# Low halves of the local attention's keys stored in both row halves, and the decode tokens' copies of 1/rms tied behind the sixth attention block

## The chip, the cores and the metric

The kernel runs on one core of one Trainium2 chip. Its time is the device time of one execution in microseconds (us). A program is timed in several runs, and the median is given. TensorE is PE in the profile (its weight loads are PEld), VectorE is DVE, ScalarE is ACT, GpSimd is POOL, and SyncE, which issues most DMAs, is SP.

## The reference, cut to what matters

One layer of a hybrid decoder: 1024 prompt tokens and 64 decode tokens (8 sequences of 8) share one input projection. Half of it feeds a retention mixer, half a sliding-window attention of 8 query heads and 2 key heads (64 wide, window 128). Output projection, residual and an MLP follow. The change touches only the attention.

```python
q_s = rms_norm(q_s.reshape(b, t, N_SWA_HEADS, HEAD_DIM), q_norm_gain)
k_s = rms_norm(k_s.reshape(b, t, N_SWA_KV, HEAD_DIM), k_norm_gain)
v_s = v_s.reshape(b, t, N_SWA_KV, HEAD_DIM)
...
# swa_prompt: each block of 128 queries reads its own and the previous block of keys
scores = jnp.einsum('bnqkgd,bnskd->bnkgqs', qb, kk).astype(jnp.float32) * (d ** -0.5)
scores = scores - slopes * dist.astype(jnp.float32)
scores = jnp.where(valid[None, :, None, None], scores, NEG_INF)
probs = sink_softmax(scores, sinks).astype(v.dtype)
out = jnp.einsum('bnkgqs,bnskd->bnqkgd', probs, vv)
```

## The kernel before, in words

**Numbers in two halves.** Most products are made of a high half in the type `fp32r` and a low half, the rest. The helper `mm3` (L178 to L180) issues three matmuls for one product: high by high, low by high, high by low. A matmul of the profile shows as rows*columns of its stationary operand, then the output: `128*128 128x256` has 128 rows of contraction, `64*128` only 64.

**The key and value stage.** For each of nine token tiles `proj_tok` issues 24 matmuls of 256 columns into `pst`. ACT squares the key part (`hsq`, L313), DVE sums and scales it (`hr`, L315, L316), POOL takes the power (`hr`, L132), DVE multiplies (L318) and makes the normed keys `kn` (L320), and PE transposes them (`ptk`, L325). For tiles 0 to 7 the transposed keys are split for each of two key heads `kv`: ACT writes the high half twice, into rows 64*kv and following and into the other 64 rows (`kh2`, L331), and DVE writes the low half once, into the rows of its own head (`kl`, L332). DVE also stores the values (L335). PSUM has two buffers for `ptk`, and three for `pst`. While this runs, PE also has the second query projection (`psq`) in its order.

**The spread of 1/rms.** When the third `rst` is known (L132), SP sends all 1088 values of 1/rms to DRAM (`r_d`, L171, L172) and loads them back into all 128 partitions (`rsb`, L173). The projections of the next stage multiply by `rsb` (L515, L524). For the decode tokens DVE makes eight small copies of one row of `rsb` (`r8s`, in the tile `q2v`, L431), which are read only by the column sums `prq8` after the attention of the prompt. In the code they stand behind the eighth attention block.

**The attention blocks.** `swa_block(c)` runs for eight blocks of 128 queries and for both key heads. `qx` holds the high half of the queries in the rows of the head (`qx[p_]`, ACT L392) and their low half in the other 64 rows (DVE L393). For each of four query heads two matmuls make the scores in one part of a PSUM bank `scp`: L400 multiplies all 128 rows of `qx` by `kh2` (high by high and low by high at once), and L401 adds the 64 high rows times the low half of the keys. DVE adds the position term (L402), the softmax follows (DVE L351 to L365, ACT L359, POOL L366), PE transposes the result (`ppp`, L371), ACT and DVE copy it out (L411, L413), PE multiplies by the values (`po`, L420), and ACT and DVE split the result (L423, L424) for the output projection.

**Order.** The program is traced in the order of the code, and a scheduler then places each engine's instructions with the times of a model; the order of an engine is fixed before the run. Between the matmuls of the attention it places those of the next projections (`psf`, `psg`), which need nothing of the attention.

Of the kernel before, what the change touches and what calls it, by code (L numbers as in the profile page):

```python
# [11 lines left out]
F32 = mybir.dt.float32  # L12
F32R = mybir.dt.float32r
AF = mybir.ActivationFunctionType
ALU = mybir.AluOpType
# [5 lines left out]
P = 128  # L21
WARM = 18
T = 1088
NB = 8
# [5 lines left out]
def tok_tile(t):  # L30
    off = 960 if t == 8 else t * 128
    c = min(off // 384, 2)
    return off, c, off - CH[c][0]
# [3 lines left out]
def hymba_layer(ctx: ExitStack, tc: tile.TileContext, a: dict, o: dict):  # L37
    nc = tc.nc
# [9 lines left out]
    def slot(i, dt, name):  # L48
        return slots.tile([P, 3072], dt, tag=f"s{i}", name=name)
# [8 lines left out]
    def cload(name):  # L58
        t_ = const.tile(list(a[name].shape), F32, name="c_" + name)
        nc.sync.dma_start(t_, a[name])  # L60
        return t_
# [43 lines left out]
    qkg = cload("qkg")  # L105
# [25 lines left out]
    def rsqrt_inplace(ap, n):  # L131
        nc.gpsimd.tensor_tensor(ap, ap, mhalf.broadcast_to([P, n]), ALU.pow)  # L132
# [68 lines left out]
    rsb = nt.tile([P, T], F32, tag="rsb", name="rsb", bufs=1)  # L201
# [5 lines left out]
    def proj_tok(t, w, ps):  # L207

        _, c, r = tok_tile(t)
        hi, lo = hn[c]  # L210
        for k in range(8):
            lh, ll = hi[:, k, r : r + 128], lo[:, k, r : r + 128]
            mm3(ps[:, :256], lh, ll, w[0][:, k, :], w[1][:, k, :], k == 0, k == 7)
        return ps


    sp = attn.enter_context(tc.tile_pool(name="swa", bufs=2))
# [15 lines left out]
    sl7, sl8 = slot(7, F32, "q2v"), None  # L233
    qs2 = sl7[:, 0:1024].rearrange("p (j n) -> p j n", j=4)
    vs = sl7[:, 1024:2048].rearrange("p (t n) -> p t n", t=8)
    q8s, r8s = (sl7[:, i : i + 512].rearrange("p (t n) -> p t n", t=4) for i in (2048, 2560))
# [60 lines left out]
        square_sum(rsb[:, 768:1088], xs[2][:, k, :], k, "m2")  # L297
    sl8 = slot(8, F32R, "kk")
    kh2 = [sl8[:, kv * 1024 : kv * 1024 + 1024] for kv in range(2)]
    kl = sl8[:, 2048:3072]  # L300
    for c, (c0, cw) in enumerate(CH):
        acc = rsb[:, c0 : c0 + cw]
        inv_rms(acc, OFFS[c], rst[:, 3 * c : 3 * c + 3], f"m{c}")
# [4 lines left out]
    for t in range(9):  # L308
        off, c, r0 = tok_tile(t)
        rt = rst[:, t : t + 1]  # L310
        ps = proj_tok(t, w, psA.tile([P, 512], F32, tag="mm", name="pst"))
        sq = sp.tile([P, 128], F32, tag="hsq", name="hsq")
        nc.scalar.activation(sq, ps[:, :128], AF.Square, scale=rt)  # L313
        r = sp.tile([P, 2], F32, tag="hr", name="hr")
        nc.vector.tensor_reduce(r, sq.rearrange("p (h d) -> p h d", h=2), AX.X, ALU.add)  # L315
        nc.vector.tensor_scalar(r, r, 1.0 / 64.0, EPS, ALU.mult, ALU.add)  # L316
        rsqrt_inplace(r, 2)
        nc.vector.tensor_scalar(r, r, rt, None, ALU.mult)  # L318
        kn = sp.tile([P, 128], F32, tag="kn", name="kn")
        nc.vector.tensor_tensor(  # L320
            kn.rearrange("p (h d) -> p h d", h=2), ps[:, :128].rearrange("p (h d) -> p h d", h=2),
            r.unsqueeze(2).broadcast_to([P, 2, 64]), ALU.mult,
        )
        pt = psB.tile([P, 512], F32, tag="t2", name="ptk")[:, :128]
        nc.tensor.transpose(pt, kn, ident)  # L325
        if t < 8:
            cols = slice(t * 128, t * 128 + 128)
            for kv in range(2):
                p_ = slice(kv * 64, kv * 64 + 64)
                for d_ in (p_, slice(64 - kv * 64, 128 - kv * 64)):  # L330
                    nc.scalar.activation(kh2[kv][d_, cols], pt[p_], AF.Copy, scale=qkg[p_, 1:2])  # L331
                nc.vector.scalar_tensor_tensor(  # L332
                    kl[p_, cols], pt[p_], qkg[p_, 1:2], kh2[kv][p_, cols].bitcast(F32), ALU.mult, ALU.subtract
                )
            nc.vector.tensor_scalar(vs[:, t, :], ps[:, 128:256], rt, None, ALU.mult)  # L335
        if t == 7:
            nc.vector.tensor_scalar(k8[:, 0:128], pt, qkg[:, 1:2], None, ALU.mult)
        if t == 8:
            nc.vector.tensor_scalar(k8[:, 128:192], pt[:, 64:128], qkg[:, 1:2], None, ALU.mult)
            nc.vector.tensor_scalar(v8, ps[64:128, 128:256], rt[64:128], None, ALU.mult)  # L340
# [27 lines left out]
    def transposed(s, j0, n, nm):  # L368
        pp = psB.tile([P, 512], F32, tag="t2", name="pp" + nm)
        for g in range(4):  # L370
            nc.tensor.transpose(pp[:n, g * 128 : g * 128 + 128], s[:, g, j0 : j0 + n], ident)  # L371
        return pp

    def mix_store(mh, ml, t0, n):
        for d_, m_ in ((ms_hi_d, mh), (ms_lo_d, ml)):
            nc.sync.dma_start(d_[:, :, t0 : t0 + n], m_[:, : 4 * n].bitcast(F32).rearrange("p (g n) -> p g n", g=4))


    def swa_block(c):
        pts = []  # L380
        mh = sp.tile([P, 512], F32R, tag="mh", name=f"mh{c}")
        ml = sp.tile([P, 512], F32R, tag="ml", name=f"ml{c}")
        k0 = max(c - 1, 0) * 128
        n = 128 if c == 0 else 256
        for kv in range(2):
            nm = f"p{c}_{kv}"
            p_ = slice(kv * 64, kv * 64 + 64)
            x_ = slice(64 - kv * 64, 128 - kv * 64)

            qx = sp.tile([P, 4, 128], F32R, tag="qx", name="qx" + nm)  # L390
            q_ = qs01[p_, :, c * 128 : c * 128 + 128] if c < 6 else qs2[p_, :, c * 128 - 768 : c * 128 - 640]
            nc.scalar.copy(qx[p_], q_)  # L392
            nc.vector.tensor_tensor(qx[x_], q_, qx[p_].bitcast(F32), ALU.subtract)  # L393
            st = sp.tile([P, 4, 256], F32, tag="s", name="s" + nm)
            s = st[:, :, 256 - n :]
            for gg in range(2):
                ps = psB.tile([P, 512], F32, tag="t1", name="sc" + nm)
                for g in (2 * gg, 2 * gg + 1):
                    pg = ps[:, (g % 2) * 256 : (g % 2) * 256 + n]
                    nc.tensor.matmul(pg, qx[:, g, :], kh2[kv][:, k0 : k0 + n], start=True, stop=False)  # L400
                    nc.tensor.matmul(pg, qx[p_, g, :], kl[p_, k0 : k0 + n], start=False, stop=True)  # L401
                    nc.vector.scalar_tensor_tensor(  # L402
                        s[:, g, :], dtab[:, 256 - n :], nsl[:, c, kv, g : g + 1], pg, ALU.mult, ALU.add
                    )
            softmax(s, n, sinks[:, 4 * kv : 4 * kv + 4], nsinks[:, 4 * kv : 4 * kv + 4], nm, rq[:, c, kv, :])
            halves = (1,) if c == 0 else (0, 1)
            pt = sp.tile([P, 2, 512], F32, tag="pt", name="pt" + nm)
            for h in halves:
                pp = transposed(st, h * 128, 128, nm)
                if h == 0:  # L410
                    nc.scalar.copy(pt[:, h, :], pp)  # L411
                else:
                    nc.vector.tensor_copy(pt[:, h, :], pp)  # L413
            pts.append(pt)

        po = psB.tile([P, 512], F32, tag="t3", bufs=1, name=f"po{c}")
        for h in halves:
            for kv in range(2):
                p_ = slice(kv * 64, kv * 64 + 64)
                nc.tensor.matmul(  # L420
                    po[p_, :], vs[:, c - 1 + h, p_], pts[kv][:, h, :], start=h == halves[0], stop=h == 1
                )
        nc.scalar.copy(mh, po)  # L423
        nc.vector.tensor_tensor(ml, po, mh.bitcast(F32), ALU.subtract)  # L424
        mix_store(mh, ml, c * 128, 128)

    for c in range(NB):
        swa_block(c)

    for c_ in range(8):  # L430
        nc.vector.tensor_copy(  # L431
            r8s[0:1, :, :].rearrange("p t (b c i) -> p t b c i", b=2, c=8)[:, :, :, c_, :],
            rsb[0:1, 1024:1088].rearrange("p (t b i) -> p t b i", t=4, b=2),
        )


    pr = psB.tile([P, 512], F32, tag="t2", name="prq8")
# [25 lines left out]
    for tt in range(2):  # L463
        ps = psB.tile([P, 512], F32, tag="t1", name="sc8")
        for t4 in (2 * tt, 2 * tt + 1):
            cc = (t4 % 2) * 192
            for new in range(2):
                for b2 in range(2):
                    b = 2 * t4 + b2
                    for kv in range(2):  # L470
                        p_ = slice(kv * 64, kv * 64 + 64)
# [12 lines left out]
    for h, n in ((0, 128), (1, 64)):  # L484
        pp = transposed(s8, h * 128, n, "s")
        pt = nt.tile([P, 512], F32, tag="ntmp", name=f"pt8{h}")
# [11 lines left out]
    mh = sp.tile([P, 512], F32R, tag="mh", name="mhs")  # L498
    ml = sp.tile([P, 512], F32R, tag="ml", name="mls")
# [375 lines left out]
    kh, kl = (sl8c[:, i : i + 512].rearrange("p (q n) -> p q n", q=4) for i in (2048, 2560))  # L875
# [372 lines left out]
```

## Time and profile before

| what | us |
|---|---|
| median of 3 runs | 1283.24 (1282.28 to 1283.95) |
| the profiled execution's own time | 1280.67 |
| its span | 1278.9 |
| PE busy in the span | 1221.7 (96%) |
| DVE, ACT, POOL busy | 838.3, 499.8, 545.7 |

A timeline row gives start, duration, engine, line, operation, names, shape and count, and in brackets how long the engine sat idle before it and what ended that. Matmuls are pipelined, so the distance from start to start, not the duration, is what one costs PE; that distance is called the pitch below. PEclk is the granted clock of TensorE, 1.00 being full speed. A row of windows gives for each engine its busy time and its number of instructions in a stretch.

### The profile page before, as it was taken

What the parts mean: (1) busy time and instruction counts of PE and PEld (TensorE: products, weight loads), DVE (VectorE), ACT (ScalarE), POOL (GpSimd) and SP (SyncE); (2) the same over time, 40 slices, a digit from 0 to 9 for tenths busy, and PEclk for the clock granted to TensorE, in tenths of its full rate; (3) what the DMA queues carried; (4) which work ended last, traced back from release to release, by engine and by line L of the source; (5) the groups of instructions that cost most, each with busy time, mean ns of one, the idle gap of its engine ahead of it and who ended that gap; (6) DMA issues with size and microseconds to landing.
All of it is one profiled execution on the core that took longest, in us unless ns stands there. A gap on an engine that the chain in (4) does not pass through costs nothing.

```text
span 1278.9 us, 23839 instructions
## 1 busy us (share of the span) xinstructions
PE 1221.7 (96%) x9621; PEld 1156.2 (90%) x9621; DVE 838.3 (66%) x1492; ACT 499.8 (39%) x1031; POOL 545.7 (43%) x463
## 2 busy tenths in 40 slices
PE   7979999999999899879999999999589999999998
PEld 5979877788979799879999999999589999999998
DVE  8735655553115787887666666766367778887766
ACT  6333343364304334444444344434264332332331
POOL 8425223123323554667565656665571321413000
PEclk9989999999989999899999999999889999999999
DMA  6211221424402944332443434333575455553124
GB/s 229 68 56 53 85 74 61 156 73 135 121 18 89 301 152 148 113 113 85 154 152 131 146 143 155 139 133 140 188 262 178 137 171 157 180 181 122 55 69 175
DMA packets 97669, 169.45 MB, mean 133 GB/s; under 512 B 11487, under 2 KB 67743, under 8 KB 97303
## 3 DMA queue, kind: packets, MB, share of 16 engines
q1 hardware_dynamic: 85783, 125.46, 29.0%
q10 hardware_dynamic: 9216, 33.56, 8.1%
q0 software_dynamic: 2560, 8.91, 2.2%
q8 instruction: 75, 1.23, 0.4%
q14 instruction: 35, 0.29, 0.1%
HBM read 114.30 MB, written 53.61 MB: 131 GB/s over the span
## 4 chain that ended last, share of the span: by engine, by line
PE 75%; DVE 9%; DMA 7%; POOL 3%; issue 3%; ACT 2%; SPq 0%; ACTq 0%; DVEq 0%; POOLq 0%
PE psd L179 8%; PE psd L180 8%; PE psd L178 8%; PE psx L178 4%; PE psx L180 4%; PE psx L179 4%; PE psf L180 3%; PE psf L178 3%; PE psf L179 3%; POOL rt L1063 2%; DMA u_d<-rt 2%; PE pst L178 2%; PE psz L178 2%; PE psz L180 2%; PE psz L179 2%
## 5 line engine op out<-in xcount | busy, mean ns | idle before, releaser
L178 PE MATMUL psd<-uh,wd_w 128*128 128x272 f32 x896 | 259.5, 290 | 17.7 <-ACT uh L754 17.7
L179 PE MATMUL psd<-uh,wd_w 128*128 128x272 f32 x896 | 260.0, 291 | 0.1
L180 PE MATMUL psd<-ul,wd_w 128*128 128x272 f32 x896 | 256.7, 289 | 0.8 <-DVE ul L755 0.8
L178 PEld LDWEIGHTS psd<-uh,wd_w 128*128 128x128 f32 x896 | 170.8, 191 | 18.1 <-ACT uh L754 18.1
L179 PEld LDWEIGHTS psd<-uh,wd_w 128*128 128x128 f32 x896 | 169.7, 189 | 0.3 <-DVE wd_w L755 0.3
L180 PEld LDWEIGHTS psd<-ul,wd_w 128*128 128x128 f32 x896 | 168.7, 189 | 1.1 <-DVE ul L755 1.1
L1118 DVE TENSOR_TENSOR a<-a,psd 128x272 f32<-128x272 f32 x248 | 102.2, 432 | 46.8 <-PE psd L180 46.7
L755 DVE TENSOR_TENSOR wu_w<-wu_s,wu_w 128x512 fp32r<-128x512 f32 x64 | 62.1, 973 | 84.6 <-ACT wu_w L754 84.4
L755 DVE TENSOR_TENSOR ul<-ur,uh 128x1088 fp32r<-128x1088 f32 x56 | 87.5, 1591 | 15.2 <-ACT uh L754 15.2
L754 ACT CAST wd_w<-wd_s 128x512 fp32r<-128x512 f32 x64 | 37.6, 621 | 112.9 <-PE psd L180 101.7
L178 PE MATMUL psx<-op_0h,wu_w 128*128 128x272 f32 x256 | 75.1, 293 | 0.7 <-ACT m L1040 0.7
L366 POOL TENSOR_TENSOR sp<-sp,ssp 128x1024 f32<-128x1024 f32 (+1 forms) x16 | 28.6, 1789 | 109.9 <-DVE ssp L365 109.9
L180 PE MATMUL psx<-op_0l,wu_w 128*128 128x272 f32 x256 | 74.3, 290 | 0.0
L178 PE MATMUL psx<-op_1h,wu_w 128*128 128x272 f32 x256 | 74.3, 290 | 0.0
L180 PE MATMUL psx<-op_1l,wu_w 128*128 128x272 f32 x256 | 74.1, 289 | 0.0
L179 PE MATMUL psx<-op_0h,wu_w 128*128 128x272 f32 x256 | 74.0, 289 | 0.0
L179 PE MATMUL psx<-op_1h,wu_w 128*128 128x272 f32 x256 | 73.7, 288 | 0.0
L754 ACT CAST uh<-ur 128x1088 fp32r<-128x1088 f32 x56 | 59.5, 1101 | 22.9 <-DMA ur<-u_d 12.4
L962 POOL TENSOR_TENSOR wd_s<-wd_r,wd_s 128x512 f32<-128x512 f32 x16 | 24.0, 1501 | 104.0 <-DVE wd_w L755 101.7
L1027 DVE SCALAR_TENSOR_TENSOR m<-m,rsf 128x272 f32<-128x272 f32 x96 | 65.5, 683 | 3.1
L180 PE MATMUL psf<-hnl,wqk_hi 128*128 128x384 f32 (+1 forms) x192 | 64.9, 338 | 0.0
L178 PE MATMUL psf<-hnh,wqk_hi 128*128 128x384 f32 (+1 forms) x192 | 64.8, 338 | 0.0
(318 smaller groups left out, 3818.8 us busy)
## 6 DMA issues: line engine op xcount, KB each, us to landing
u_d<-rt SPq DMA_DIRECT2D x32, 952.0 KB, 6.1
ur<-u_d SPq DMA_DIRECT2D x56, 544.0 KB, 5.0
wu_r<-in_w_up ACTq DMA_DIRECT2D x32, 512.0 KB, 4.3
wd_r<-in_w_down ACTq DMA_DIRECT2D x32, 512.0 KB, 5.9
y<-in_xY POOLq DMA_DIRECT2D x16, 272.0 KB, 3.3
y_d<-y POOLq DMA_DIRECT2D x16, 272.0 KB, 3.7
yt<-y_d SPq DMA_DIRECT2D x16, 272.0 KB, 3.3
out_yT<-a SPq DMA_DIRECT2D x16, 272.0 KB, 2.2
```

The source lines that it names most:

```text
L178: nc.tensor.matmul(ps, lh, rh, start=first, stop=False, skip_group_check=more)
L179: nc.tensor.matmul(ps, ll, rh, start=False, stop=False, skip_group_check=more)
L180: nc.tensor.matmul(ps, lh, rl, start=False, stop=last, skip_group_check=more)
L366: nc.gpsimd.tensor_tensor(s, s, ss.unsqueeze(2).broadcast_to([P, 4, n]), ALU.mult)
L754: nc.scalar.copy(hi, src)
L755: lo_eng.tensor_tensor(lo, src, hi.bitcast(F32), ALU.subtract)
L962: nc.gpsimd.tensor_tensor(t_, p_, q_, op)
L1027: nc.vector.scalar_tensor_tensor(t_, src, 0.0, rsf[:, s, h, :], ALU.max, ALU.mult)
L1063: sub = lambda o_, p_, q_: nc.gpsimd.tensor_tensor(o_, p_, q_, ALU.subtract)
L1118: nc.vector.tensor_tensor(to, to, ps, ALU.add)
```

## The change

Three edits. First, the low halves of the keys get a tile of 128 rows for each key head (`kl2`; the second is a new tile of 4 KB in each partition), and DVE writes each low half twice, as ACT does with the high half. Second, L401 multiplies all 128 rows of `qx` by it; so the product of low by low, which was left out before, is added. Third, the eight copies L431 are put behind the last DVE instruction of the sixth block, by an order on DVE alone and without a semaphore.

```diff
-    kl = sl8[:, 2048:3072]
+    kl2 = [sl8[:, 2048:3072], sp.tile([P, 1024], F32R, tag="kl", name="kl", bufs=1)]
...
                 for d_ in (p_, slice(64 - kv * 64, 128 - kv * 64)):
                     nc.scalar.activation(kh2[kv][d_, cols], pt[p_], AF.Copy, scale=qkg[p_, 1:2])
-                nc.vector.scalar_tensor_tensor(
-                    kl[p_, cols], pt[p_], qkg[p_, 1:2], kh2[kv][p_, cols].bitcast(F32), ALU.mult, ALU.subtract
-                )
+                    nc.vector.scalar_tensor_tensor(
+                        kl2[kv][d_, cols], pt[p_], qkg[p_, 1:2], kh2[kv][p_, cols].bitcast(F32), ALU.mult, ALU.subtract
+                    )
...
                     nc.tensor.matmul(pg, qx[:, g, :], kh2[kv][:, k0 : k0 + n], start=True, stop=False)
-                    nc.tensor.matmul(pg, qx[p_, g, :], kl[p_, k0 : k0 + n], start=False, stop=True)
+                    nc.tensor.matmul(pg, qx[:, g, :], kl2[kv][:, k0 : k0 + n], start=False, stop=True)
...
-        nc.vector.tensor_tensor(ml, po, mh.bitcast(F32), ALU.subtract)
+        ins = nc.vector.tensor_tensor(ml, po, mh.bitcast(F32), ALU.subtract)
         mix_store(mh, ml, c * 128, 128)
-
-    for c in range(NB):
-        swa_block(c)
-
-    for c_ in range(8):
-        nc.vector.tensor_copy(
-            r8s[0:1, :, :].rearrange("p t (b c i) -> p t b c i", b=2, c=8)[:, :, :, c_, :],
-            rsb[0:1, 1024:1088].rearrange("p (t b i) -> p t b i", t=4, b=2),
-        )
+        return ins
+
+    done_swa = [swa_block(c) for c in range(NB)]
+    with tc.issue_after(done_swa[5].ins):
+        for c_ in range(8):
+            nc.vector.tensor_copy(
+                r8s[0:1, :, :].rearrange("p t (b c i) -> p t b c i", b=2, c=8)[:, :, :, c_, :],
+                rsb[0:1, 1024:1088].rearrange("p (t b i) -> p t b i", t=4, b=2),
+            )
```

In DVE's order of before, in the key and value stage, the copies L431 stand around the first steps of token tile 4 (L315 to L320 are its norm, `q2v<-pst` its values, `kk<-ptk` low halves of keys):

```order
L332 SCALAR_TENSOR_TENSOR kk<-ptk,c_qkg,kk 64x128
L431 COPY q2v<-rsb 1x8x8 x4
L315 TENSOR_REDUCE hr<-hsq 128x2
L431 COPY q2v<-rsb 1x8x8 x4
L316 TENSOR_SCALAR hr<-hr 128x2
L332 SCALAR_TENSOR_TENSOR kk<-ptk,c_qkg,kk 64x128
L318 TENSOR_SCALAR hr<-hr,rst 128x2
L320 TENSOR_TENSOR kn<-pst,hr 128x128
L335 TENSOR_SCALAR q2v<-pst,rst 128x128
```

The same place in DVE's order of the change, token tile 4 again:

```order
L315 TENSOR_REDUCE hr<-hsq 128x2
L332 SCALAR_TENSOR_TENSOR kk<-ptk,c_qkg,kk 64x128
L316 TENSOR_SCALAR hr<-hr 128x2
L332 SCALAR_TENSOR_TENSOR kl<-ptk,c_qkg,kk 64x128
L332 SCALAR_TENSOR_TENSOR kk<-ptk,c_qkg,kk 64x128
L318 TENSOR_SCALAR hr<-hr,rst 128x2
L320 TENSOR_TENSOR kn<-pst,hr 128x128
L335 TENSOR_SCALAR q2v<-pst,rst 128x128
L332 SCALAR_TENSOR_TENSOR kl<-ptk,c_qkg,kk 64x128
```

The copies are gone from here, and four writes of low halves (`kk` and `kl`) stand for each token tile where two stood. On ACT the number of writes is the same, but each now has one of DVE's behind it on the same PSUM tile. In PE's order 206 matmuls stand between the first and the ninth transpose `ptk` in both kernels, 144 of 256 columns (`pst`) and 62 of 384 (`psq`); the transposes stand a little further apart, the last three more so.

The place in DVE's order of the change where the copies now stand is behind L424 of the sixth block; L353 and L402 belong to the two blocks behind it, and `gst` is a projection:

```order
L351 TENSOR_REDUCE mxp_1_1974<-sp_1_1959 128x4
L424 TENSOR_TENSOR ml_1806<-po_1899,mh_1805 128x512
L431 COPY q2v<-rsb 1x8x8 x8
L353 TENSOR_TENSOR mxp_1_1974<-mxp_1_1974,rq 128x4
L413 COPY ptp_0_1943<-ppp_0_1950 128x512
L402 SCALAR_TENSOR_TENSOR sp_0_2016<-dtab,nsl,scp_0_2017 128x256
```

All eight stand together there, with the softmax of a later block behind them. Behind the attention the orders of all engines are nearly the same as before; SP's stores and loads in the attention change places among each other.

## The prediction

> **What bounds the kernel now.** I read the busy shares and the chain of waits first, to see which engine carries the end, then windows of the two places that the edits touch, and there the waits and the timeline.
>
> ```profile
> PE 1221.7 (96%) x9621; PEld 1156.2 (90%) x9621; DVE 838.3 (66%) x1492; ACT 499.8 (39%) x1031; POOL 545.7 (43%) x463
> PE 75%; DVE 9%; DMA 7%; POOL 3%; issue 3%; ACT 2%; SPq 0%; ACTq 0%; DVEq 0%; POOLq 0%
> 60.00:80.00 20.00, 13.35 (x97) 13.15 (x96) 7.98 (x36) 7.09 (x20) 2.79 (x4) 0.83 0.08 29
> 75.03:79.46 4.43, 4.43 (x21) 4.43 (x22) 3.25 (x14) 2.55 (x7) 1.39 (x2) 0.52 0.01 4
> 100.00:320.00 220.00, 220.00 (x1367) 179.36 (x1366) 118.22 (x278) 89.50 (x214) 70.11 (x33) 1.00 0.28 93
> ```
>
> The first line is the page's busy times, the second its chain by engine, the rest windows (length, then PE, PEld, DVE, ACT, POOL, granted clock, DMA). PE is the bound: 96% busy and 75% of the chain. In the attention, 100 to 320 us, it is busy in all 220 us while DVE has 118, so time saved on PE there is time saved. In the key and value stage there is a hole: 13.35 of 20 us, and just behind it a clock of 0.52.
>
> **The hole.** A row of waits (total, times, longest) and timeline rows.
>
> ```profile
> PE ptk L325 <- DVE kn L320: 6.7, 1, 6.7
> 72.38 0.49 DVE L431 COPY q2v<-rsb 1x64 f32<-1x64 f32 x4 [9.21 <-DMA rsb<-r_d]
> 106.00 0.56 DVE L515 TENSOR_TENSOR qkst<-psf,rsb 128x384 f32<-128x384 f32 x1 [0.73 <-PE psf L180]
> 67.98 0.28 PE L179 MATMUL pst<-wkv_hi,hnl 128*128 128x256 f32 x1
> 68.10 0.28 PE L180 MATMUL pst<-wkv_lo,hnh 128*128 128x256 f32 x1
> 75.03 0.47 PE L325 MATMUL ptk<-c_ident,kn 128*128 128x128 f32 x1 [6.65 <-DVE kn L320]
> 75.16 0.56 PE L178 MATMUL pst<-wkv_hi,hnh 128*128 128x256 f32 x1
> 79.49 0.36 PE L180 MATMUL pst<-wkv_lo,hnh 128*128 128x256 f32 x1
> ```
>
> DVE works in order, and L431 stands there 9.2 us until the 1/rms come back from DRAM. Behind it are queued the norm and `kn` of token tile 4, for which PE's transpose waits: PE starts nothing from 68.10 to 75.03. The third edit takes L431 out of this place. Nothing else there needs `rsb`: its next reader, L515, stands behind the whole stage (at 106.00 before, where `rsb` had landed by 72.38). What is late next is the norm itself, weighed below.
>
> The gain: from 68.10 to 79.49 are 11.4 us. The window from 75.03 holds 21 PE instructions, one the transpose; 20 matmuls of 256 columns at the pitch of 0.12 us (67.98 to 68.10) plus one for 68.10 are 2.5 us, two transposes some 0.2. **11.4 - 2.7 = 8.7 us**: 6.7 of waiting and 2.0 of half speed. That the clock comes back too is safe only if no other hole opens.
>
> **The 64-row matmul.** Timeline of PE in the attention, with its weight loads below:
>
> ```profile
> 182.73 0.33 PE L180 MATMUL psf<-hnl,wqk_hi 128*128 128x384 f32 x1
> 182.91 0.34 PE L178 MATMUL psf<-hnh,wqk_hi 128*128 128x384 f32 x1
> 183.08 0.28 PE L400 MATMUL scp<-kk,qxp 128*128 128x256 f32 x1
> 183.29 0.38 PE L401 MATMUL scp<-kk,qxp 64*128 64x256 f32 x1
> 183.60 0.45 PE L179 MATMUL psf<-hnh,wqk_lo 128*128 128x384 f32 x1
> 183.88 0.28 PE L400 MATMUL scp<-kk,qxp 128*128 128x256 f32 x1
> 184.09 0.38 PE L401 MATMUL scp<-kk,qxp 64*128 64x256 f32 x1
> 184.40 0.45 PE L180 MATMUL psf<-hnl,wqk_hi 128*128 128x384 f32 x1
> 184.69 0.34 PE L178 MATMUL psf<-hnh,wqk_hi 128*128 128x384 f32 x1
> 182.91 0.19 PEld L400 LDWEIGHTS scp<-kk,qxp 128*128 128x128 f32 x1
> 183.29 0.18 PEld L401 LDWEIGHTS scp<-kk,qxp 64*128 64x128 f32 x1 [0.19 <-issue]
> 183.60 0.19 PEld L179 LDWEIGHTS psf<-hnh,wqk_lo 128*128 128x128 f32 x1
> L401 PE MATMUL scp<-kk,qxp x64: 323/380/383, 103.0 to 293.1; 64*128 64x256 f32 x56, 64*128 64x128 f32 x8
> ```
>
> The load of L400 starts at 182.91, a matmul ahead of its use; the 64-row load of L401 and the full one behind it start only with their own matmuls. So L400 holds 0.21 us where full-height neighbours of 256 columns take 0.12, L401 0.31, and the 384-column matmul behind 0.28 to 0.29 where 0.175 is usual (182.73 to 182.91). From 183.08 to 184.69 are 1.61 us for four matmuls of 256 columns and two of 384; at the usual pitch 4 x 0.12 + 2 x 0.175 = 0.83. The excess is 0.78 for two, **0.39 us for each L401**, and there are 64 (last row): **25.0 us**. With `kl2` all are 128 rows high. The gain lies between 0 (the price stays) and 25; I take all of it, since the nearest rows are those of `pst`, 256 columns, full height, 0.12 apart with loads as long as here.
>
> The Trainium skill, on "TensorE: Matmul & The Clock Gate", in "Why this matters for your kernels", holds that a single matmul of few rows of contraction takes as long as one of 128. By that the second edit would be worth nothing and the sum only 8.7 us; the trace differs, since L401 holds PE for 0.31 us where 0.12 is usual.
>
> **What is added.** 16 more L332, and each key tile's four writes on ACT now alternate with four on DVE, since both read one PSUM tile and wait for each other:
>
> ```profile
> 57.01 0.74 ACT L331 ACTIVATE kk<-ptk,c_qkg 64x128 fp32r<-64x128 f32 x2 [2.66 <-PE ptk L325]
> 57.78 0.34 DVE L332 SCALAR_TENSOR_TENSOR kk<-ptk,c_qkg,kk 64x128 fp32r<-64x128 f32 x1 [0.28 <-ACT kk L331]
> 58.16 0.74 ACT L331 ACTIVATE kk<-ptk,c_qkg 64x128 fp32r<-64x128 f32 x2 [0.41 <-DVE kk L332]
> 61.30 0.70 POOL L132 TENSOR_TENSOR hr<-hr,mhalf 128x2 f32<-128x2 f32 x1 [3.48 <-DVE hr L316]
> 62.98 0.37 ACT L313 ACTIVATE hsq<-pst,rst 128x128 f32<-128x128 f32 x1 [0.40 <-PE pst L180]
> L335 DVE TENSOR_SCALAR q2v<-pst,rst 128x128 f32<-128x128 f32 x6 | 2.1, 342 | 0.0
> L320 DVE TENSOR_TENSOR kn<-pst,hr 128x128 f32<-128x128 f32 x7 | 2.0, 292 | 0.6
> L315 DVE TENSOR_REDUCE hr<-hsq 128x2 f32<-128x128 f32 x6 | 1.7, 277 | 2.2 <-ACT hsq L313 2.1
> L318 DVE TENSOR_SCALAR hr<-hr,rst 128x2 f32<-128x2 f32 x7 | 1.6, 229 | 2.4 <-POOL hr L132 2.3
> L431 DVE COPY q2v<-rsb 1x64 f32<-1x64 f32 x8 | 1.0, 175 | 9.2 <-DMA rsb<-r_d 9.2
> ```
>
> A step is 0.37 on ACT, 0.35 on DVE and 0.04 for each handover (57.75 to 57.78, 58.12 to 58.16): 0.80, so 3.2 us for the four of a tile. PE's own work is 144 x 0.12 + 62 x 0.175 + eight transposes at some 0.1 = 28.9 us for the eight tiles, 3.6 each. The rest of DVE's work on a tile (0.34, 0.29, 0.28, 0.23 and L316, as small as L318: 1.3 to 1.4 us) and ACT's `hsq` (0.37) fall in the other engine's turns. So the chain stays 0.4 us a tile shorter than PE's work: cost **0**. From the other side, if nothing overlaps at all, a tile takes 3.2 + 1.4 + 0.37 + 0.70 on POOL = 5.6 us, and eight take 45, **16 us** more than PE's work. I take 0, since tiles overlap in the order; 16 goes into the range. Behind the waiting writes stands the next tile's norm, hence PE's transpose.
>
> The copies L431 cost 1.0 us in their new place. Behind them there stand L353 and L413 of a later block; DVE is idle for some 46% of that stretch (118 of 220), so 0 to 1.0, taken as 0. Their reader, the column sums, comes a block and a half later.
>
> **Does the attention keep up?** A PE that is faster by 25 us over 16 rounds gets 1.6 us earlier in each to what the other engines make.
>
> ```profile
> 192.05 1.90 POOL L366 TENSOR_TENSOR sp<-sp,ssp 128x1024 f32<-128x1024 f32 x1 [6.11 <-DVE ssp L365]
> 199.76 0.49 PE L371 MATMUL ppp<-c_ident,sp 128*128 128x128 f32 x3
> PEld scp L400 <- DVE ptp L413: 0.8, 1, 0.8
> PEld scp L400 <- DVE sp L402: 0.8, 1, 0.8
> ```
>
> The softmax is ready at 193.95, and PE takes it at 199.76, 5.8 us later; 1.6 us less leaves most. Waits of PE's loads for DVE in the attention are two of 0.8 us; I add as much again, **1.6 us**, with bounds 0 and 25 (all the gain turns into waiting).
>
> **Sum.** 25.0 + 8.7 - 1.6 = 32.1 us. The profiled execution took 1280.67, so it becomes 1248.6; it lies 2.6 below the median of 1283.24, and with the same offset the forecast is **1251**.
>
> **Rivals.**
> 1. The chain of ACT and DVE becomes the bound of the key stage. For it: eight handovers a tile where four were, and POOL in the norm. Against: 3.2 against 3.6 us. Up to 16 us: 1257 to 1267.
> 2. The attention's chain takes PE's place. For it: the order was made by a model, not by this trace. Against: 5.8 us in hand. Half the gain lost gives 1251 + 12 = 1263, all of it 1276.
> 3. The edit of the scores does not do what it says: the price belongs to the pair, not to the 64 rows. For it: L400 and L401 share a bank and a stationary operand. Against: no other full-height pair shows it. Only the hole is won: 1283.2 - 8.7 + 1.6 = 1276. The Trainium skill's rule on few rows, above, leads here too.
> 4. Slower than before. Two full loads on the same rows cannot overlap a running matmul: each waits for the end of the matmul before (0.28) and then loads (0.19), 0.47 for each of the pair, and 0.28 + 0.19 = 0.47 again before the next one instead of 0.175. That is an excess of 2 x 0.35 + 0.3 = 1.0 for each pair, 0.61 above now, 39 us in all, less 8.7: some 1313. It decides from an excess above 0.39 + 8.7/64 = 0.53 us. Against: `pst` at 0.12. The same page of the Trainium skill, in "Part 3: Packing small matmuls" under "What overlaps and what doesn't", says that loads overlap running matmuls only where the row groups differ; by that rule this rival would hold. The trace disagrees: loads of 0.19 us on all 128 rows keep a pitch of 0.12.
>
> **How the numbers follow.** Forecast 0.74 (1246 to 1257), first rival 0.10, second 0.08, third 0.05, fourth 0.02, the rest, with no change, 0.01. The low end, 1246, is the full gain without the 1.6 us, 1249.5, less the scatter of runs and some pairs with an excess of 0.41; the high end, 1267, takes in the first rival's bound and the milder half of the second. About 0.2% (2.6 us) is what a measurement of this kernel can tell from no change: faster 0.97, same 0.01, slower 0.02.
>
> **What would show it.** Right: L431 no longer waits, the transposes `ptk` wait for less than 1 us each, the clock stays at 1.00 from 60 to 95 us, L401 reads 128*128, and pairs stand 0.12 apart. Wrong on the first term: a new wait of PE for `kn` in the same stage. Wrong on the second: a pitch above 0.2 at L401, or new waits of L400, L371 and L420 in the attention. What would make the whole wrong is a later stage that now ends on a DMA and gives back the lead.

## The result, and the profile after

| | us |
|---|---|
| before, median of 4 runs | 1282.76 (1281.40 to 1283.95) |
| after, median of 4 runs | 1253.33 (1252.94 to 1255.31) |
| ratio | 0.9774, 95% interval 0.9757 to 0.9791 |
| profiled execution, before and after | 1280.67 and 1253.02 |

The kernel is 29.4 us faster by the medians and 27.65 by the two profiled executions; the forecast was 1251, from a sum of 32.1. The busy times and the chain of the page after:

```profile
PE 1198.9 (96%) x9621; PEld 1151.8 (92%) x9621; DVE 841.5 (67%) x1508; ACT 504.4 (40%) x1035; POOL 545.3 (44%) x463
PE 59%; DMA 6%; DVE 5%; POOL 4%; ACT 3%; issue 2%; ACTq 0%; SPq 0%; POOLq 0%; DVEq 0%
```

Two windows of after, with the columns of the prediction's:

```profile
60.00:80.00 20.00, 20.00 (x156) 19.96 (x155) 14.60 (x50) 12.31 (x31) 7.30 (x7) 1.00 0.12 36
100.00:320.00 220.00, 216.35 (x1519) 191.89 (x1518) 121.54 (x285) 102.87 (x235) 80.70 (x42) 0.99 0.33 104
```

PE issues as many instructions as before in 22.8 us less of busy time. The key stage has no hole any more (20.00 of 20 us at full clock, against 13.35 at 0.83). From 100 to 320 us PE is no longer busy throughout: 3.65 of 220 us are idle, 1.9 of them behind the attention, at 313 us. Groups of after: the copies, the transposes of the keys and the last products of the decode tokens' attention (count, then ns min/median/max, first and last start):

```profile
L431 DVE COPY q2v<-rsb x8: 174/176/177, 247.3 to 248.0; 1x64 f32<-1x64 f32 x8
L325 PE MATMUL ptk<-c_ident,kn x9: 270/271/327, 56.6 to 85.4; 128*128 128x128 f32 x9
L495 PE MATMUL po<-pt,smp x32: 222/223/243, 309.0 to 309.9; 128*64 128x32 f32 x32
```

The timeline of PE in after, at two pairs of scores:

```profile
172.31 0.28 PE L400 MATMUL scp<-kk,qxp 128*128 128x256 f32 x1
172.43 0.28 PE L401 MATMUL scp<-kl,qxp 128*128 128x256 f32 x1
172.55 0.28 PE L400 MATMUL scp<-kk,qxp 128*128 128x256 f32 x1
172.67 0.28 PE L401 MATMUL scp<-kl,qxp 128*128 128x256 f32 x1
172.78 0.31 PE L180 MATMUL psf<-hnl,wqk_hi 128*128 128x320 f32 x1
```

The copies stand at 247 us and wait for nothing. The pairs stand 0.12 us apart, and a projection follows after another 0.11: the height of 64 rows and its price are gone.

The same two groups of before tell how the gain grows along the way:

```profile
L325 PE MATMUL ptk<-c_ident,kn x9: 270/272/473, 56.6 to 94.0; 128*128 128x128 f32 x9
L495 PE MATMUL po<-pt,smp x32: 222/223/243, 336.9 to 337.8; 128*64 128x32 f32 x32
```

After is 8.6 us ahead at the last transpose (94.0 to 85.4) and 27.9 at the last L495, with 20 more matmuls of the value projection (2.4 us) already done by then: 30.3. Of that some is given up at once. Three of PE's waits between 40 and 420 us (what waited, for whom, us in total, times, longest):

```profile
PE pst L178 <- ACT vtr L578: 2.3, 2, 1.9
PE po L420 <- ACT ptp L411: 1.1, 1, 1.1
PE scp L400 <- DVE sp L402: 0.5, 2, 0.3
```

The timeline of after at the first of these, and the window around it:

```profile
312.92 1.20 ACT L578 ACTIVATE vtr<-pst,rst 128x256 f32<-128x256 f32 x3 [2.34 <-DMA ms_hi_d<-mhs]
313.45 0.39 PE L178 MATMUL pst<-wv_hi,hnh 128*128 128x256 f32 x1 [1.91 <-ACT vtr L578]
314.26 0.41 PE L178 MATMUL pst<-wv_hi,hnh 128*128 128x256 f32 x1
314.47 0.42 PE L179 MATMUL pst<-wv_hi,hnl 128*128 128x256 f32 x1
```

```profile
310.00:320.00 10.00, 8.09 (x58) 7.85 (x55) 0.42 (x1) 2.05 (x5) 3.19 (x5) 0.83 0.72 203
```

Two more in this stretch, of `rsr` for `qkb`, are 3.4 us, and 3.6 in before; one of 1.8 us, of `pso` for the weights `woa`, does not come back in a second profiled execution of the change. The waits of the attention for ACT and DVE are 1.6 us, none in before. Behind the attention the first copies of the values (`vtr`, L578) wait for the store `ms_hi_d` to read `mhs`, whose memory they take over; the three `pst` buffers are full, PE waits 1.9 us, and some 15 matmuls behind it run 0.21 apart instead of 0.12, another 1.4 us. In before the same copies waited 3.02 us for a store and PE only 0.19.

### The profile page after: what moved, and what is told of

It is laid out like the page before. It is cut to its first block, busy times and chain, and to the rows that moved or that the text cites. A ratio compares the mean times of both kernels' runs of the same rounds, so it can differ in the third digit from the quotient of the medians.

```text
span 1251.2 us, 23864 instructions
## 1 busy us (share of the span) xinstructions
PE 1198.9 (96%) x9621; PEld 1151.8 (92%) x9621; DVE 841.5 (67%) x1508; ACT 504.4 (40%) x1035; POOL 545.3 (44%) x463
## 4 chain that ended last, share of the span: by engine, by line
PE 59%; DMA 6%; DVE 5%; POOL 4%; ACT 3%; issue 2%; ACTq 0%; SPq 0%; POOLq 0%; DVEq 0%
PE psd L179 9%; PE psd L180 9%; PE psd L178 9%; PE psx L178 3%; PE psx L179 3%; PE psx L180 3%; DMA u_d<-rt 3%; POOL rt L1063 3%; PE psz L180 2%; PE psz L179 2%; PE psz L178 2%; PE pst L178 1%; PE pst L179 1%; PE pso L179 1%; PE pso L180 1%
## 5 line engine op out<-in xcount | busy, mean ns | idle before, releaser
L366 POOL TENSOR_TENSOR sp<-sp,ssp 128x1024 f32<-128x1024 f32 (+1 forms) x16 | 28.6, 1787 | 100.4 <-DVE ssp L365 95.7
L754 ACT CAST uh<-ur 128x1088 fp32r<-128x1088 f32 x56 | 59.5, 1099 | 21.7 <-DMA ur<-u_d 11.3
```

Of the source, the lines that this page charges most:

```text
L366: nc.gpsimd.tensor_tensor(s, s, ss.unsqueeze(2).broadcast_to([P, 4, n]), ALU.mult)
L754: nc.scalar.copy(hi, src)
```

## The experiments

All ratios are to the kernel before, which was timed anew beside each group of runs: 1282.77 us beside each edit alone, the writes in pairs and the first kernel with other memory; 1281.66 beside the zero half, the grouped rows, the writes twice and the pairs with other memory; 1284.25 beside the last two. These three lie up to 2.6 us apart, and a difference in us between kernels of two groups can be off by as much. Line numbers in the rows of an experiment can be a few above those of the change.

### Each edit alone

The first two edits without the third: the copies go back behind the last block.

```diff
-    done_swa = [swa_block(c) for c in range(NB)]
-    with tc.issue_after(done_swa[5].ins):
-        for c_ in range(8):
+    for c in range(NB):
+        swa_block(c)
+    for c_ in range(8):
```

> The first two edits alone; the copies L431 stay where they were. My theory (both prices are separate and add up): the hole of 6.65 us with its 2 us of half clock stays, and the change's 29.4 us shrink by some 8.7, so 1261 to 1264, a ratio of 0.983 to 0.985 to the kernel before; L431 waits some 9 us for rsb again. Rival (the copies matter little, since the keys' low halves now keep DVE busy there anyway, or the lead is lost later as it was behind the attention): 1253 to 1256. Rival (the hole was the greater part): above 1268.

Measured: 1257.87 us, ratio 0.9801 (0.9784 to 0.9818), 24.9 us less than before. Then the third edit alone:

```diff
-                    nc.tensor.matmul(pg, qx[:, g, :], kl2[kv][:, k0 : k0 + n], start=False, stop=True)
+                    nc.tensor.matmul(pg, qx[p_, g, :], kl[p_, k0 : k0 + n], start=False, stop=True)
```

> The third edit alone; low halves and L401 as before. My theory: 8.4 to 8.7 us go at the end of the key stage and stay gone, 1274 (ratio 0.993); L401 still 64*128, with an excess of 0.35 to 0.39 us each. Rival (the lead is given back later, in the attention's waits or behind it): 1279 to 1282. If the two edits need each other, this run and the one with the rows alone do not add up to the change's 29.4 us.

Measured: 1273.33 us, ratio 0.9921 (0.9901 to 0.9940), 9.4 us less. Two waits in the key stage of the first of the two:

```profile
PE pst L178 <- DVE q2v L335: 6.7, 1, 6.7
DVE q2v L432 <- DMA rsb<-r_d: 9.1, 1, 9.1
```

Its window of that stage, and its groups of the transposes and of the decode tokens' last products:

```profile
60.00:80.00 20.00, 13.28 (x98) 12.99 (x97) 8.83 (x37) 6.22 (x18) 2.09 (x3) 0.86 0.09 28
```

```profile
L325 PE MATMUL ptk<-c_ident,kn x9: 270/272/415, 57.1 to 95.4; 128*128 128x128 f32 x9
L496 PE MATMUL po<-pt,smp x32: 222/223/243, 315.6 to 316.5; 128*64 128x32 f32 x32
```

The same window of the copies alone, and its group L401:

```profile
60.00:80.00 20.00, 20.00 (x156) 19.96 (x155) 12.15 (x41) 13.60 (x35) 7.79 (x7) 1.00 0.14 48
```

```profile
L401 PE MATMUL scp<-kk,qxp x64: 323/380/383, 94.0 to 285.0; 64*128 64x256 f32 x56, 64*128 64x128 f32 x8
```

With the copies in their old place the hole is back to the tenth of a microsecond, and with it the lower clock; with the copies moved and the low halves as before, the hole is gone and the 64-row matmuls are there. So each price belongs to its edit. But 24.9 + 9.4 = 34.3 us, and the change has 29.4: **together they lose some 4.9 us** that each alone does not. (Each of the three has an interval of some 2 us to either side, and in its second timing, below, the change has 30.4; so the loss is clear, its size is not sharp.) The rows alone came out 3 to 6 us faster than expected. From the last transpose to the last L495 it takes 221.1 us, the change 224.5; 1.6 of these 3.4 us are 13 more matmuls of the value projection that the change does by then.

The traces show where the two edits lose it. The last transposes of the retention stage, in the kernel before, the change, the rows alone and the copies alone:

```profile
L734 PE MATMUL pm<-c_ident,mixtok x4: 222/222/272, 490.6 to 490.8; 64*128 64x64 f32 x4
L734 PE MATMUL pm<-c_ident,mixtok x4: 222/222/273, 465.7 to 465.9; 64*128 64x64 f32 x4
L735 PE MATMUL pm<-c_ident,mixtok x4: 222/222/272, 470.1 to 470.3; 64*128 64x64 f32 x4
L734 PE MATMUL pm<-c_ident,mixtok x4: 222/222/273, 484.5 to 484.7; 64*128 64x64 f32 x4
```

By then PE has done the same matmuls in the last three, and in before 25 fewer of the output projection (3.1 us at 0.125). So the leads are 28.0 us for the change, 23.6 for the rows and 9.2 for the copies, and 23.6 + 9.2 - 28.0 = 4.8: in these executions the loss is complete here, nearly 800 us ahead of the end. Most of it lies behind the attention. From the last L495 to this point the rows alone take 153.8 us, the change 156.0 although it has the 1.6 us of projections behind it: 3.8 us more.

### Is it the height of the operand?

The other half of each `kl2` is filled with zeros once, and DVE writes the low halves once, as before the change:

```diff
+    for kv in range(2):
+        x_ = slice(64 - kv * 64, 128 - kv * 64)
+        nc.scalar.activation(kl2[kv][x_], rsb[x_, 0:1024], AF.Copy, scale=0.0)
...
-                    nc.vector.scalar_tensor_tensor(
-                        kl2[kv][d_, cols], ...
+                nc.vector.scalar_tensor_tensor(
+                    kl2[kv][p_, cols], ...
```

> The change, but the other row half of each kl2 holds zeros, written once by ACT ahead of the stage, and DVE writes each low half once, as before the change. So the product of low by low is left out, as it was before. L401 reads 128 rows. My theory (the price hangs on the height of L401's operands, not on what is in them, and the 16 added writes are not what the gain costs or brings): L401 stands 0.12 us from its neighbours, and the time is between that of the change and that of the writes in pairs, 1248 to 1254. Rival (the added writes hold up the key stage): below 1247. Rival (the price has to do with the data or with a tile shared by both heads): the 0.35 to 0.39 us for each L401 come back, 1270 or more.

Measured: 1249.59 us, ratio 0.9744 (0.9723 to 0.9765). Its timeline on PE, where L403 and L404 are L400 and L401; the next projection starts at 125.23:

```profile
125.00 0.28 PE L403 MATMUL scp<-kk,qxp 128*128 128x256 f32 x1
125.11 0.28 PE L404 MATMUL scp<-kk,qxp 128*128 128x256 f32 x1
```

Zeros do as well as numbers: L401 wins by having 128 rows, not by what is in them. Then the 64-row matmuls of before, with the third edit, but two of a kind behind each other:

```diff
+                for g, pg in pgs.items():
+                    nc.tensor.matmul(pg, qx[:, g, :], kh2[kv][:, k0 : k0 + n], ...)
+                for g, pg in pgs.items():
+                    nc.tensor.matmul(pg, qx[p_, g, :], kl[p_, k0 : k0 + n], ...)
```

> The third edit with L401 of 64 rows as before the change, but the four matmuls of a bank stand as L400, L400, L401, L401 instead of L400, L401, L400, L401; the computation is the same. It stands against the copies alone (1273.3 us). Theory A (the price is that of a change of height, from 128 to 64 rows and back, some 0.39 us for each way there and back): half the changes, so 12 us less, 1260 to 1263. Theory B (the price is that of every matmul with 64 rows): no difference, 1272 to 1275. The pitch in the trace tells too: by A the second L401 of a pair stands 0.12 us behind the first, by B 0.2 to 0.31.

Measured: 1262.01 us, ratio 0.9838 (0.9812 to 0.9865), 11.3 us less than the copies alone, or 10.2 with each held against its own timing of before. (Unlike what the expectation says, the attention scores are changed. The sums of the two heads of a bank are begun one inside the other here, and part of them is probably lost by that, which is not shown. Number, size and kind of the instructions are the same.) Its timeline on PE; L402 is L401 here, and a row x2 is two matmuls:

```profile
172.74 0.34 PE L178 MATMUL psf<-hnh,wqk_hi 128*128 128x384 f32 x1
172.91 0.40 PE L400 MATMUL scp<-kk,qxp 128*128 128x256 f32 x2
173.24 0.50 PE L402 MATMUL scp<-kk,qxp 64*128 64x256 f32 x2
173.66 0.44 PE L179 MATMUL psf<-hnh,wqk_lo 128*128 128x384 f32 x1
173.94 0.33 PE L180 MATMUL psf<-hnl,wqk_hi 128*128 128x384 f32 x1
```

The second 64-row matmul by itself, and its load:

```profile
173.46 0.28 PE L402 MATMUL scp<-kk,qxp 64*128 64x256 f32 x1
173.34 0.19 PEld L402 LDWEIGHTS scp<-kk,qxp 64*128 64x128 f32 x1
```

From 172.91 to 173.94 are 1.03 us; at the usual pitch, 4 x 0.12 + 0.175, it would be 0.66. The excess is 0.37 for two 64-row matmuls, where the prediction found 0.78. **Two 64-row matmuls behind each other cost together what one alone costs**, so the price is not one for each of them, and theory A has the time (12 us expected, 10 to 11 measured). Its sign in the trace is not there, though: by A the second should stand 0.12 us behind the first, and it stands 0.22 behind (173.24 to 173.46), as B has it. The excess is spread over the stretch, some 0.1 us on each of four starts. What a third in the row would cost no run shows.

### Do the added writes cost?

Half as many handovers between ACT and DVE, with the same instructions:

```diff
                 for d_ in (p_, slice(64 - kv * 64, 128 - kv * 64)):
                     nc.scalar.activation(kh2[kv][d_, cols], ...)
+                for d_ in (p_, slice(64 - kv * 64, 128 - kv * 64)):
                     nc.vector.scalar_tensor_tensor(kl2[kv][d_, cols], ...)
```

> The change, but for each key head ACT writes both high halves and then DVE both low halves, so the engines change places half as often on each PSUM tile; the same instructions otherwise. My theory (the chain of ACT and DVE is hidden behind PE in the key stage): the same time, 1252 to 1255, and the key stage's last transpose within 0.5 us of the change's 85.6 us. Rival (the handovers cost PE something): 1 to 3 us faster, and seen before 90 us.

Measured: 1248.32 us, ratio 0.9731 (0.9717 to 0.9746), 5.0 us less than the change, with intervals that don't meet. Both theories missed: it is faster, but not in the key stage. Its windows of the key stage and of the attention, then the change's own window of the attention:

```profile
60.00:80.00 20.00, 20.00 (x159) 19.96 (x158) 15.40 (x52) 13.25 (x34) 6.01 (x7) 1.00 0.12 33
100.00:310.00 210.00, 209.96 (x1438) 186.34 (x1436) 120.38 (x281) 96.19 (x228) 75.26 (x38) 1.00 0.31 100
```

```profile
100.00:310.00 210.00, 208.26 (x1467) 184.04 (x1465) 121.12 (x284) 100.82 (x230) 77.51 (x38) 1.00 0.31 99
```

The groups of transposes and last products with the writes in pairs:

```profile
L325 PE MATMUL ptk<-c_ident,kn x9: 270/271/327, 57.5 to 86.5; 128*128 128x128 f32 x9
L496 PE MATMUL po<-pt,smp x32: 222/223/243, 306.0 to 306.9; 128*64 128x32 f32 x32
```

The last transpose comes 1.1 us later than in the change and the last L495 3.0 earlier, with 13 fewer matmuls of the value projection done by then (1.6 us). PE is as busy in the key stage as can be in both. In the attention PE has 0.04 us idle here and 1.7 in the change: the scheduler laid out another order, in which the waits for `sp` and `ptp` don't arise. More is won behind it. The last transposes of the retention stage, with the same matmuls done on PE as in the change:

```profile
L735 PE MATMUL pm<-c_ident,mixtok x4: 222/222/273, 459.7 to 459.9; 64*128 64x64 f32 x4
```

That is 6.0 us ahead of the change: 1.1 lost in the key stage, 2.5 won in the attention (220.4 us against 222.9 without the 1.6) and 4.6 between the last L495 and this point (153.0 against 157.6 with them). The two profiled executions end 3.1 us apart, so part of it is given back later there. The sum of the two edits alone, 34.3 us, is what this order gives (1282.77 - 1248.32 = 34.4). Then the writes twice:

```diff
-                    nc.vector.scalar_tensor_tensor(kl2[kv][d_, cols], ...)
+                    for _ in range(2):
+                        nc.vector.scalar_tensor_tensor(kl2[kv][d_, cols], ...)
```

> The change, with each L332 issued twice (64 in all where the change has 32), the second time with the same result. The turns of ACT and DVE on one PSUM tile become 4 x (0.37 + 0.70 + 0.08) = 4.6 us for a token tile, against PE's 3.6. If that chain bounds the stage once it is longer than PE's work, as the prediction's first rival has it: the last transpose ptk some 8 us later than in the change (85.4), the end 1260 to 1262. If DVE's turns overlap with something that the prediction took as serial: less than 3 us, 1253 to 1256. It tells how near the change stands to that bound: its own chain was put at 3.2 against 3.6 us.

Measured: 1261.56 us, ratio 0.9834 (0.9811 to 0.9858), 8.2 us more than the change (9.3 with each held against its own timing of before): the number of the chain theory. The trace tells another way to it. A window of the writes twice, its group of transposes, and two of its waits:

```profile
310.00:320.00 10.00, 4.07 (x45) 2.89 (x44) 2.05 (x5) 0.54 (x3) 2.45 (x3) 0.71 0.11 25
```

```profile
L325 PE MATMUL ptk<-c_ident,kn x9: 270/271/328, 57.4 to 92.8; 128*128 128x128 f32 x9
```

```profile
PE pst L178 <- ACT vtr L579: 3.6, 2, 3.3
PE pps L372 <- POOL s L367: 2.1, 1, 2.1
```

The stage is longer by 7.4 us (92.8 against 85.4; some 8 were expected), but PE waits for 0.3 us only in it (for `kl`, at a transpose): the scheduler put 38 more projections ahead of the last transpose (100 in place of 62 beside the 144 of `pst`), and these fill the 7.4 us. New waits come later: at 310 us PE is busy for 4.07 of 10 us. So a longer chain of ACT and DVE did lengthen the key stage, by way of the order, and the price is seen in another stage. That those waits come because the 38 are missing there as filler is likely, but not shown.

### The wait at 313 us

Three kernels aim at the first `vtr`. In the first, the split of the decode tokens' output lies in other memory, so that `vtr` need not wait for the store to read it:

```diff
-    mh = sp.tile([P, 512], F32R, tag="mh", name="mhs")
-    ml = sp.tile([P, 512], F32R, tag="ml", name="mls")
+    mh, ml = (sl6[:, i : i + 256].bitcast(F32R) for i in (2816, 2048))
```

> The change, but the split of the decode tokens' attention output (the mh and ml ahead of the value projections) lies in other memory, so that the first copy vtr (L578) no longer needs the memory that the store ms_hi_d is still reading. In the change vtr waits 2.34 us for it, PE 1.91 us, and PE then runs at half clock for some 3.2 us. Theory (this wait is where 3 to 4 us of the lead go): PE's wait at 313 us and the clock's fall go, and the end comes 3 to 4 us earlier, 1249.5 to 1250.5. Rival (another transfer ends at the same time, since vtr's memory has more than one reader, or the lead is given back further on): 1252.5 to 1254.

Measured: 1251.40 us, ratio 0.9759 (0.9743 to 0.9775), between what the theory and the rival have. The second adds this to the writes in pairs:

> The writes in pairs and the split of the decode tokens' attention output in other memory, together. With the writes in pairs PE waits only 0.35 us for the first vtr. Theory (both repair the same loss, the wait at vtr; with the pairs there is nothing left for the other to win): 1247 to 1249, no difference to the pairs alone. Rival (they repair different losses and add up): 1245 to 1246.5.

Measured: 1251.63 us, ratio 0.9766 (0.9751 to 0.9781): 3.3 us slower than the pairs alone (4.4 with each held against its own timing of before), which neither theory has. In the third, filler is kept back for the wait:

```diff
+            with tc.issue_after(behind) if k >= k0 else ExitStack():
                 mm3(ps[:, :256], lh, ll, w[0][:, k, :], w[1][:, k, :], k == 0, k == 7)
...
+                proj_tok(t, w_v[i], ps, last_po8.ins, 3)
```

> The change, with the last 15 of the 24 matmuls of the third value tile tied behind the last L495 on PE; the attention of the prompt stands as in the change. So 47 matmuls of pst stand ahead of the last L495, where the change has 62. All runs so far fit one rule: the three pst buffers hold 72 matmuls, so 72 less those ahead remain as cover, and PE's wait at the first vtr is 3.1 us less 0.12 for each of them (change: 10 remain, 1.9; the rows alone and the writes in pairs: 23 remain, 0.35; the writes twice: none remain, 3.3). Theory (this cover is what the change lost): 25 remain, a wait of 0 to 0.2 us, no fall of the clock at 313 us, and 3 to 3.5 us less than the change: 1249 to 1251. Rival (what is won there is lost again some us later, as with the other memory): 1251.5 to 1254.

Measured: 1252.99 us, ratio 0.9768 (0.9748 to 0.9788), beside it the change once more:

> The change itself once more, beside the kernel with 15 matmuls tied behind: the same time as in its first timing, 1252 to 1255, with PE's wait of 1.9 us at the first vtr and a granted clock below 0.9 behind it.

Measured: 1253.83 us, ratio 0.9767 (0.9747 to 0.9787). By its number the rival has it; but the two kernels' runs overlap (1252.15 to 1255.27 and 1251.18 to 1255.76), and 3 us can't be ruled out. A window of the kernel with 15 matmuls kept back, two of its waits, and one of the kernel with other memory:

```profile
310.00:320.00 10.00, 9.90 (x81) 9.70 (x82) 0.42 (x1) 2.53 (x6) 3.14 (x4) 1.00 0.79 219
```

```profile
PE pst L180 <- POOL wv_lo L79: 1.0, 1, 1.0
PE pur L700 <- DVE kdr L632: 1.4, 1, 1.4
```

```profile
PE pur L694 <- DVE kdr L626: 1.7, 1, 1.7
```

The wait and the fall of the clock are gone, as foreseen, and nothing is won that the runs can tell. With filler kept back, the attention ends no sooner (309.8), in part because PE now meets a wait for `wv_lo` ahead of L495. And in the retention stage all three kernels have a wait of `pur` for `kdr` (1.4 to 1.7 us) that the change and the writes in pairs don't have. It is not the lead that opens it: the kernel before has one of 1.3 us, and the zero half, which starts the retention stage 0.9 us earlier than the kernel with other memory (324.7 and 325.6), has none. That the order of each kernel decides it is likely, but not shown. At the last transposes of the retention stage, with the 25 matmuls of the output projection allowed for that these two have not done by then, the kernel with other memory is 2.3 us ahead of the change (460.5) and the one with filler kept back 0.8 behind (463.6).

## Why the prediction was right, and where it was off

The mechanism was right for the hole and in the main for the 64-row matmul, and the sum 32.1 against 29.4 measured. By the two traces, up to the end of the retention stage, 8.6 us came from the hole, 23.3 from the 64-row matmuls, and 1.6 were lost in the attention and 2.3 behind it: 28.0.

- **The hole.** Forecast 8.7 us. The last transpose came 8.6 us earlier in the change, and the third edit alone won 9.4. DVE's next work came in time, and the clock stayed at 1.00. Right.
- **The 64-row matmul.** Forecast 25.0 us. From the last transpose to the last L495 are 243.8 us before and 224.5 after; with the 2.4 us of projections done ahead and the 1.6 of new waits taken out, 23.3. The rows alone won 24.9. Nearly right in size. The price was put on each L401, though, and two L401 behind each other cost no more than one: in before each stood alone among full-height matmuls. That no two did is what made 64 times the price right.
- **The added writes.** Forecast 0, bound 16. (Ten of the 62 `psq` matmuls have 320 columns and stand 0.15 us apart, so PE's work is 28.6 us and not 28.9; nothing hangs on it.) In the change PE has no wait in the key stage, so the stage itself paid nothing. As a term of the sum it was too narrow: the writes go into the scheduler's order, and two ways to issue the same writes lie 5.0 us apart, all of it behind the stage. The first rival's mechanism, PE waiting in the key stage, came to 0.3 us even with the writes doubled, though the stage became longer.
- **The waits of the attention.** Forecast 1.6 us; 1.6 measured. That the numbers meet is luck: the forecast doubled two waits of weight loads for DVE, and 1.1 of what came is `po` waiting for a copy of ACT. A new wait at L420 was even one of the prediction's signs of being wrong; here it was small.
- **What would make the whole wrong.** The prediction ended on a later stage that ends on a DMA. That happened, in a small way: 1.9 us of waiting at the first `vtr` and 1.4 at the lower clock. What the sum lacked is a term for what stands behind the attention: from the last L495 to the end of the retention stage the change takes 156.0 us, before 153.7 with the same matmuls to do, 2.3 us. The writes in pairs, with the same matmuls done, lose nothing there and have all of 34.4 us. Whether the wait at `vtr` is what costs the change this time the runs don't show: two kernels without it (other memory, filler kept back) are 1.9 us faster than the change's first median and 0.8 than its second, less than the 3.3, and within the scatter. Which moves of the order carry the 5 us stays open.
- **The rivals.** The third, that the price belongs to the pair in one bank, falls with the change's own pairs and the zero half: full-height pairs in one bank stand 0.12 apart. The rule of the Trainium skill, "TensorE: Matmul & The Clock Gate", "Why this matters for your kernels", that a single matmul of few rows takes as long as one of 128, does not carry over to this stream: among full-height neighbours the 64-row matmul costs 0.39 us more. Whether the rule holds for a matmul by itself no run here shows. The fourth needed an excess of 0.53 us for each L401 in its new form; the pairs stand 0.12 apart.

## What to carry to other kernels

Where a stream of full-height matmuls is broken by ones with half the rows, read the pitch from start to start, not the durations, and count how often they break it: fill the missing rows (zeros will do) or put the low ones together (here two cost as much as one). A small copy that waits for a DMA in an engine's fixed order holds up all that is queued behind it; look at what that engine owes to the bound one. And where a scheduler lays out the order, a rewrite that leaves the work alone can move the time by as much as the edit's last few microseconds, so try more than one form. And a hole that one sees in a trace is not yet time won: two ways to close the 1.9 us at 313 us won nothing that the runs can tell.

## What was not expected of the hardware

**The clock differs between executions of one kernel.** Two profiled executions of the change, in the same stretch without a wait of PE, first and second timing:

```profile
329.40:349.40 20.00, 20.00 (x145) 15.97 (x144) 6.19 (x10) 1.54 (x3) 5.84 (x6) 0.83 0.00 1
```

```profile
329.40:349.40 20.00, 20.00 (x139) 16.75 (x140) 5.49 (x9) 1.54 (x3) 5.40 (x5) 0.74 0.00 1
```

From the first `rsr` to the last L676, the same work in both, it takes 27.0 us in the first (329.5 to 356.5) and 28.4 in the second (329.3 to 357.7): 1.4 us. A share of the scatter between runs (1251.18 to 1255.76 in five of the change) may come from this.

**Two loads on all 128 rows stand 0.12 us apart** although each takes 0.19. The load's group in the change:

```profile
L401 PEld LDWEIGHTS scp<-kl,qxp x32: 187/188/192, 111.8 to 267.6; 128*128 128x128 f32 x32
```

So there a load overlaps matmuls and another load that use the same rows. The Trainium skill's page named above lets loads overlap running matmuls only where their row groups differ ("Part 3: Packing small matmuls", "What overlaps and what doesn't"); here loads on the same rows do overlap, and it is at a change of height that the overlap stops: in the grouped rows the second 64-row load starts 0.12 us ahead of its matmul (173.34 and 173.46), while the loads at the two changes start with theirs.
